# A two-layer trunk in one kernel: where residual tiles land, when prepared weight parts are made, and when attention's value products run

## The chip, the cores and the metric

The kernel is one program on one core of a Trainium2 chip. The time is the device time of one execution in microseconds (us). Before the change it is 2508.14 us, the median of three runs (2506.28 to 2510.22). In this document TensorE is the engine of the matrix products (PE in the profile), VectorE is DVE, ScalarE is ACT, GpSimd is POOL, and SyncE is SP, which here only issues transfers. PSUM is the memory that TensorE writes, SBUF the one from which all engines read.

## The reference

1024 tokens of width 1024 pass two layers. Each layer is a mixer, a multilayer perceptron (MLP) and a gated embedding (ple), each with a root-mean-square norm ahead of it and the residual added behind it. Layer 0's mixer is a gated spatial unit beside a gated delta rule; the change does not touch it. Layer 1's is differential attention with 8 heads, two sub-heads of 64 dimensions each, and values of 128. Cut to what matters:

```python
for layer in range(2):
    hn = rms_norm(h, ln_mix[layer])
    if layer == 0:
        h = h + concatenate([gmlp(hn), gated_delta(hn)]) @ w_out_e
    else:
        q, k, v = split(hn @ w_qkv_o)            # 8 heads; q, k normed per sub-head
        logits = q_r @ k_r.T - slope * dist      # r = 0, 1; causal
        attn = softmax(logits_0) - lam * softmax(logits_1)
        h = h + rms_norm(attn @ v) @ w_out_o
    hn = rms_norm(h, ln_mlp[layer])
    h = h + square(relu(hn @ w_mlp1[layer])) @ w_mlp2[layer]    # 1024 -> 4096 -> 1024
    gate = sigmoid(rms_norm(h, ln_ple[layer]) @ w_ple_gate[layer])
    h = h + (p[layer] @ w_ple_proj[layer]) * gate
```

All of it is in 32-bit floats.

## The kernel before

**Products.** Activations lie with the feature on the partitions, in tiles of 128 x 512: 8 tiles of features (m, or k where they are summed over), 2 halves of 512 tokens. Each operand x is split into two shorter numbers, hi = cast(x) on ACT and lo = x - hi on DVE (`split`, L265 and L269), and one product is three matmuls, hi·hi, hi·lo and lo·hi (`mm3`, which issues at L81; transposes are L84). A weight is loaded by SP into a `raw` buffer (8 of them, used in turn), its two parts go to `w` buffers (12, in turn). A buffer taken again waits for whoever still reads its old content.

**MLP.** Each of its two matrices is a 2 x 2 block product done with seven block products instead of eight. The first matrix runs in 8 chunks of columns: `front(0..4)` makes two products of chunks 0 to 4, `rest(0..4)` the other five of each of them, `chained(5..7)` all seven of the last three, with sums on DVE, relu and square on ACT. The hidden activations go to DRAM (`gd`). The second matrix is seven calls of `product2`, n = 1, 5, 6, 3, 7, 4, 2, each with 16 steps; a step loads 256 KB of weights (`raw` or `keep`) and 256 KB of `gd` (`graw`), splits both, and issues 12 matmuls of 128 x 512.

**Prepared parts.** Beside the first layer's MLP runs a generator, `prepare` (`side` in the code). One `next` of it is a step; there are 32, 8 heads by 4 pieces of the query and key weights. A step has POOL load a `raw` buffer (2 transfers of 128 KB, L243), ACT and DVE split it, and POOL store the two parts in DRAM (`qk_dram`, 256 KB each). Attention loads them from there. Eight steps run behind chunks 5 to 7 (3, 3 and 2), and 24 in the odd steps of the products n = 1, 4 and 2.

**Regions.** Large tiles have fixed places in SBUF, and one place serves many stages. A0 holds the values of two heads during attention; A2 and A3 the keys, of even and odd heads; A4, A5 and A1 the logits, in turn; c0 to c13 are 128 x 512 places, of which c8 to c10 hold `aT`, transposed probabilities. Afterwards A0 to A3 take the residual tiles `acc` of layer 1: 8 tiles of features for each half, four to a region.

**Attention.** The 64 blocks are 8 heads by 8 blocks of 128 queries. Step g of the loop issues, in this order: the logits of sub-head 0 of block g; the combination of the two probabilities of block g-1; transposes of the next queries (`put_q`); the transposes of block g-2 (`tr`, then a copy to `aT` on ACT); the logits of sub-head 1 of block g; the value products of block g-2 (`po`). Between these are four calls of `pump`, which put in other matmuls: projections of later heads' queries and keys (112 units), and from call 210 on the output matrix's sums over the first heads (`tails`, `mix_part`). KA = (5,5) says that the first five heads are summed there for each half of the tokens, in tiles `res` that are then written back to the residual in DRAM, `h_dram`. Behind the loop `mix_out` sums the other three heads: for each tile SP loads `acc` from `h_dram`, TensorE makes the sum, DVE adds it (L1496) and ACT squares it for the next norm.

**What sets the order.** The program's order is only the start: the tiling framework schedules the instructions with a simulation of its own and fixes each engine's order from that. SP and POOL take their transfers strictly in that order, so a transfer that waits for a buffer holds up all that stand behind it on the same engine.

Of the kernel before, what the change touches and what calls it, by code (L numbers as in the profile page):

```python
# [11 lines left out]
F32 = mybir.dt.float32  # L12
F32R = mybir.dt.float32r
AF = mybir.ActivationFunctionType
# [4 lines left out]
P = 128  # L19
# [4 lines left out]
HT = 512  # L24
# [4 lines left out]
WB = 12  # L29
EARLY = 3000  # L30
LAG = 3
KA = (5,5)
NQK = 112
MARKS = ((224, NQK),)
TAIL = 210
# [9 lines left out]
def f32(ap):  # L45
    return ap.bitcast(F32)
# [92 lines left out]
class Trunk:  # L139
# [192 lines left out]
    def mlp(self, x, x_tags, gain, w1, w2, gain_next, h_dram, p, last, side=iter(())):  # L332
        nc = self.nc
# [213 lines left out]
        t3, t2, make_t4, make_t1 = operands()  # L547
        for c in range(NCH):
            (rest if c < 5 else chained)(c)
            if c > 4:  # L550
                for _ in itertools.islice(side, 3 - (c == 7)):
                    pass
            if c + 2 in away:
                for i, t in enumerate(itertools.chain(*places(c + 2))):
                    nc.sync.dma_start(t, away[c + 2][i])
            elif c == 3:
                open1(5)
                open2(5)


        pT = self.split_p(p)
# [43 lines left out]
        def product2(n, ps, new=False, beside={}):  # L605

            for kt in range(NK):
                if kt in beside:
                    beside[kt]()
                if n in (1, 2, 4) and kt % 2:  # L610
                    next(side, None)
                a = self.parts(left(n, kt), nc.vector)
                raw = self.slot(f"c{next(raws)}", [P, HT], F32, "graw")
                load(raw, gd[n - 1][kt // 2][kt % 2])
                if n == 1 and kt < 4:
                    b = self.hs_parts(0, 4 + kt)
# [527 lines left out]
    def attention(self, w_qkv, v_dram, w_out, gain_next, h_dram):  # L1144

        nc = self.nc
        NB = NT
# [63 lines left out]
        lgs = [self.slot(t, [P, 2, S], F32, "lg") for t in ("A4", "A5", "A1")]  # L1211
        lg0, lg1 = ([x[:, r] for x in lgs] for r in range(2))
        qk_tag = itertools.cycle(("aux", "sc", "aux"))
        aT_tag = itertools.cycle(("c8", "c9", "c10"))
        heads = {}

        def begin(hd):

            qk = qks[hd]

            ks = self.slot(f"A{2 + hd % 2}", [P, 2, S], F32R, "ks")

            def put_k(hf):
                pt = self.aux([P, HT], "tr", "tr")
                for t in range(4):
                    self.pe.transpose(pt[:, t * P : (t + 1) * P], qk[1][hf][:, t, :], self.ident)
                for r in range(2):
                    own, other = half[r], half[1 - r]
                    dst = ks[:, r, hf * HT : (hf + 1) * HT]
                    nc.scalar.activation(dst[own], pt[own], AF.Copy, scale=self.kg[own])  # L1230
                    nc.vector.scalar_tensor_tensor(dst[other], pt[own], self.kg[own], f32(dst[own]), ALU.mult, ALU.subtract)

            def put_q(b2):
                pt = self.aux([P, HT], "tr", "tr")
                for i in range(2):
                    self.pe.transpose(pt[:, i * P : (i + 1) * P], qk[0][b2 // 2][:, 2 * (b2 % 2) + i, :], self.ident)
                qh = self.slot(f"c{11 + b2 % 2}", [P, 2, 2 * P], F32R, "qh")
                ql = qlow[b2 % 2]
                for r in range(2):
                    own, other = half[r], half[1 - r]  # L1240
                    g = self.qg[own, hd : hd + 1]
                    nc.scalar.activation(qh[own, r], pt[own, 0 : 2 * P], AF.Copy, scale=g)
                    nc.scalar.activation(qh[other, r], pt[own, 0 : 2 * P], AF.Copy, scale=g)
                    nc.vector.scalar_tensor_tensor(ql[own, r], pt[own, 0 : 2 * P], g, f32(qh[own, r]), ALU.mult, ALU.subtract)
                return qh, ql

            put_k(0)
            heads[hd] = [ks, put_k, put_q, put_q(0)]

        class Block:  # L1250
# [38 lines left out]
            def transpose(me):  # L1289
                me.aT = []  # L1290
                for c in range((me.n + HT - 1) // HT):
                    k0, k1 = 4 * c, min(me.b + 1, 4 * c + 4)
                    pt = self.aux([P, HT], "tr", "tr")
                    for k in range(k0, k1):
                        self.pe.transpose(pt[:, (k - k0) * P : (k - k0 + 1) * P], me.lg[0][:, k * P : (k + 1) * P], self.ident)
                    me.aT.append(self.slot(next(aT_tag), [P, HT], F32, "aT"))
                    nc.scalar.copy(me.aT[c][:, : (k1 - k0) * P], pt[:, : (k1 - k0) * P])  # L1297

            def value(me):
# [100 lines left out]

        tail = tails()
        blocks = []
        for g in range(8 * NB + 2):
            if g % NB == 2 and 0 < g // NB < 7:
                values(g // NB + 1)
            if g < 8 * NB:
                hd, b = divmod(g, NB)
                blocks.append(Block(hd, b))
                blocks[g].logits(0)
            if 0 < g <= 8 * NB:  # L1410
                blocks[g - 1].combine()
            pump()
            if g < 8 * NB and b % 2 and b < NB - 1:
                q = heads[hd][2]((b + 1) // 2)
            if g > 1:
                blocks[g - 2].transpose()
            pump()
            if g < 8 * NB:
                if b == 3 - (hd < 7):
                    heads[hd][1](1)  # L1420
                blocks[g].logits(1)
            pump()
            if g > 1:
# [832 lines left out]
def trunk(tc, x, p, ln_mix_e, w_in_e, gmlp_v_gain, gmlp_ws, gmlp_bs, gdn_conv, gdn_a_log, gdn_dt_bias, gdn_out_gain,  # L2256
          w_out_e, ln_mix_o, w_qkv_o, attn_q_gain, attn_k_gain, diff_lambda, attn_sub_gain, w_out_o, ln_mlp, w_mlp1,
          w_mlp2, ln_ple, w_ple_gate, w_ple_proj, masks, out):
    with ExitStack() as ctx:
# [60 lines left out]
        for layer in range(2):  # L2320
# [18 lines left out]
            acc, pT = T.mlp(x, (("A0", "A1") if layer else ("A1", "A0"), ("A2", "A3")), gain[3 * layer + 1], w_mlp1[layer], w_mlp2[layer], gain[3 * layer + 2], h_dram, p[layer, 0], layer == 1, T.prepare(w_qkv_o[0]) if layer == 0 else iter(()))  # L2339
# [50 lines left out]
```

## Time and profile before

| | us |
|---|---|
| median of three runs | 2508.14 (2506.28 to 2510.22) |
| the profiled execution | 2509.59 |
| its span, from the first to the last instruction | 2507.9 |
| TensorE busy in it | 2486.3 |
| DVE, ACT, POOL busy in it | 1828.3, 1347.9, 283.3 |

The mean TensorE clock granted in it is 0.998 of full speed. In the span, layer 0's mixer takes up to about 478 us, the first MLP's first matrix up to 790, its second up to 1101, the gated embedding and the values up to 1290, attention up to 1728, the rest of its output matrix up to 1768, the second MLP up to 2388, the last gated embedding up to 2508.

In rows of waits, `PE mm L81 <- DVE acc L1496: 4.7, 1, 4.7` would read: TensorE's matmuls into tiles `mm` waited 4.7 us in all, once, at most 4.7, and DVE's instruction at L1496 that writes `acc` ended that wait. In rows of windows the stretch comes first, then its length and the busy time (and count) of TensorE's matmuls, TensorE's weight loads, DVE, ACT and POOL, then the granted clock, the busy share of the 16 DMA engines and what they moved in GB/s. Rows of the chain give a start, a length, and the work in it. Rows of groups give the busy time, the mean length of one in ns, and the idle time ahead of them with who ended it. Ends of matmuls are modelled, so two in a row overlap in the rows.

### The profile page before, as it was taken

To read this page: it belongs to the slowest core of one execution; us is meant where nothing else is said; L and a number is where in the kernel's file an instruction comes from. 1 tells how busy PE (TensorE), PEld (TensorE's weight loads), DVE (VectorE), ACT (ScalarE), POOL (GpSimd) and SP (SyncE) were. 2 spreads that over 40 slices of the span, in tenths; PEclk is the share of its full clock that TensorE was granted. 3 is DMA by queue.
4 is the path that set the end of the run, shared out by engine and by line. 5 is a ranking of instruction groups with operands and counts; after the bars stand their busy time and mean duration, and the time that the engine had idled before them with its cause. 6 is when DMAs were issued, how large, how long until landed. Compare 5 with 4: busy or idle time off the path is not lost. (4 is left out here: it accounts for less than half of the span.)

```text
span 2507.9 us, 39353 instructions
## 1 busy us (share of the span) xinstructions
PE 2486.3 (99%) x13465; PEld 2112.4 (84%) x13465; DVE 1828.3 (73%) x3548; ACT 1347.9 (54%) x2734; POOL 283.3 (11%) x331
## 2 busy tenths in 40 slices
PE   9999999999999999999999999999999999999999
PEld 7898998888887888888889999987888888888887
DVE  7867665787666877766847787776887656788576
ACT  6635473655555444644527777764654555445452
POOL 0211220000023001410012333310000000000000
PEclk9999999999999999999999999999999999999999
DMA  8464445467569757964451221376467548656651
GB/s 237 129 183 106 151 124 168 158 215 242 182 232 354 268 165 231 314 187 147 149 182 54 89 73 60 132 238 195 154 219 227 189 163 294 202 186 205 198 175 64
DMA packets 326386, 454.05 MB, mean 181 GB/s; under 512 B 48836, under 2 KB 168104, under 8 KB 326184
## 3 DMA queue, kind: packets, MB, share of 16 engines
q1 hardware_dynamic: 317432, 425.82, 52.8%
q0 software_dynamic: 8192, 25.17, 3.0%
q8 instruction: 106, 1.74, 0.3%
q14 instruction: 96, 0.79, 0.1%
q10 hardware_dynamic: 560, 0.53, 0.1%
HBM read 318.23 MB, written 133.18 MB: 180 GB/s over the span
## 5 line engine op out<-in xcount | busy, mean ns | idle before, releaser
L81 PE MATMUL mm<-g,w 128*128 128x512 f32 x2592 | 603.2, 394 | 4.4 <-DVE g L269 4.4
L265 ACT CAST w<-raw 128x512 fp32r<-128x512 f32 (+1 forms) x588 | 359.8, 617 | 453.1 <-PE mm L81 381.7
L81 PEld LDWEIGHTS mm<-g,w 128*128 128x128 f32 x2592 | 487.6, 188 | 118.9 <-DVE g L269 5.2
L81 PE MATMUL mm<-hi,w 128*128 128x512 f32 x1728 | 554.5, 396 | 1.0 <-DVE g L339 0.7
L269 DVE TENSOR_TENSOR w<-raw,w 128x512 fp32r<-128x512 f32 (+1 forms) x588 | 399.2, 687 | 190.9 <-ACT w L265 168.1
L81 PE MATMUL mm<-w,hi 128*128 128x256 f32 (+2 forms) x2112 | 440.9, 302 | 1.4 <-DVE k L1195 0.9
L81 PEld LDWEIGHTS mm<-hi,w 128*128 128x128 f32 x1728 | 324.2, 188 | 76.0 <-ACT w L265 1.3
L81 PEld LDWEIGHTS mm<-w,hi 128*128 128x128 f32 x2112 | 339.2, 188 | 19.1 <-DVE k L1195 2.0
L81 PE MATMUL mm<-lo,w 128*128 128x512 f32 x864 | 340.3, 394 | 0.0
L81 PE MATMUL mm<-w,lo 128*128 128x256 f32 (+2 forms) x1056 | 316.2, 300 | 0.0
L81 PE MATMUL mm<-t,w 128*128 128x512 f32 x1152 | 271.3, 394 | 0.0
L81 PEld LDWEIGHTS mm<-t,w 128*128 128x128 f32 x1152 | 216.5, 188 | 50.5
L81 PEld LDWEIGHTS mm<-w,lo 128*128 128x128 f32 x1056 | 198.9, 188 | 7.9
L81 PEld LDWEIGHTS mm<-lo,w 128*128 128x128 f32 x864 | 162.5, 188 | 36.2
L269 DVE TENSOR_TENSOR g<-graw,g 128x512 fp32r<-128x512 f32 x216 | 148.1, 687 | 11.8 <-ACT g L265 6.1
L265 ACT CAST g<-graw 128x512 fp32r<-128x512 f32 x216 | 132.8, 618 | 37.6 <-PE mm L81 16.0
L310 POOL TENSOR_TENSOR r<-ms,mhalf 128x4 f32<-128x4 f32 x12 | 14.2, 1186 | 968.0 <-DVE ms L308 935.0
L1279 ACT ACTIVATE lg<-lg,nm 128x128 f32<-128x128 f32 (+7 forms) x128 | 99.4, 778 | 39.0 <-DVE nm L1276 37.9
L405 ACT ACTIVATE g<-g 128x512 f32<-128x512 f32 x100 | 63.1, 632 | 68.3 <-DVE g L339 68.0
L243 POOL DMA_DIRECT2D raw<-in_w_qkv_o_dram x64 | 46.4, 727 | 412.0 <-DMA gd<-v 207.5
L81 PE MATMUL mm<-ohi,w 128*128 128x512 f32 x256 | 86.6, 407 | 4.7 <-DVE acc L1496 4.7
L1276 DVE CUSTOM_DVE_ANT_0 lg<-qk,al 128x512 f32<-128x512 f32 (+3 forms) x128 | 74.4, 586 | 20.4 <-PE qk L81 18.3
(382 smaller groups left out, 3744.5 us busy)
## 6 DMA issues: line engine op xcount, KB each, us to landing
raw<-in_w_mlp_dram SPq DMA_DIRECT2D x352, 256.0 KB, 3.6
graw<-gd SPq DMA_DIRECT2D x224, 256.0 KB, 3.0
gd<-g SPq DMA_DIRECT2D x192, 256.0 KB, 3.6
raw<-in_w_ple_gate_dram SPq DMA_DIRECT2D x76, 256.0 KB, 3.6
acc<-h_dram SPq DMA_DIRECT2D x64, 256.0 KB, 5.0
qk_dram<-w POOLq DMA_DIRECT2D x64, 256.0 KB, 5.5
keep<-in_w_mlp_dram SPq DMA_DIRECT2D x64, 256.0 KB, 5.5
w<-qk_dram SPq DMA_DIRECT2D x64, 256.0 KB, 3.9
```

What stands on the lines that cost most here:

```text
L81: self._next(self.engine.matmul(*a, **k))
L243: self.nc.gpsimd.dma_start(raw[:, :, j * P : (j + 1) * P], w_qkv[2 * i * P : 2 * (i + 1) * P, c : c + P].rearrange("(k p) m -> p k m", p=P))
L265: inst = self.nc.scalar.copy(hi, src)
L269: inst = (lo_engine or self.nc.vector).tensor_tensor(lo, src, f32(hi), ALU.subtract)
L310: nc.gpsimd.tensor_tensor(r, ms, self.mhalf[:, 0:4], ALU.pow)
L405: nc.scalar.activation(g, src, AF.Relu)
L1276: nc.vector.tensor_tensor_reduce(out=lg[:, k0:k1], in0=ps[:, : k1 - k0], in1=al[:, u0 + k0 : u0 + k1], scale=-0.5 ** (hd + 1), scalar=3.0e ...
L1279: nc.scalar.activation(lg[:, :n], lg[:, :n], AF.Exp, bias=nm[:, r, nch - 1 : nch], scale=-1.0, accum_out=me.sums[:, b, r : r + 1])
```

## The change

It has four parts. Residual tiles: attention's output sums take the first six heads instead of five for half 0, and layer 1's residual tiles go to the regions A2, A0, A1, A3 in this order instead of A0, A1, A2, A3; the second MLP names the regions accordingly. Prepared parts: four steps behind each of chunks 1 to 4 of the first matrix (16), and 16 in the odd steps of the products n = 4 and 2; none behind chunks 5 to 7 and none in n = 1. Value products: those of block g-3 instead of g-2, issued ahead of the transposes of the next queries, with one more step of the loop, the load of the next head's values one step later, and five places instead of three for `aT` (two small places, rb0 and rb1, are added). Queries: in `put_q` the copies to the other half of the partitions come behind both first copies and their subtractions.

```diff
-KA = (5,5)
+KA = (6,5)
+ACC = "A2", "A0", "A1", "A3"
...
             (rest if c < 5 else chained)(c)
-            if c > 4:
-                for _ in itertools.islice(side, 3 - (c == 7)):
+            if 0 < c < 5:
+                for _ in itertools.islice(side, 4):
                     pass
...
-                if n in (1, 2, 4) and kt % 2:
+                if n in (2, 4) and kt % 2:
                     next(side, None)
...
-        aT_tag = itertools.cycle(("c8", "c9", "c10"))
+        aT_tag = itertools.cycle(("c8", "c9", "c10", "rb0", "rb1"))
...
                 for r in range(2):
-                    own, other = half[r], half[1 - r]
+                    own = half[r]
                     g = self.qg[own, hd : hd + 1]
                     nc.scalar.activation(qh[own, r], pt[own, 0 : 2 * P], AF.Copy, scale=g)
-                    nc.scalar.activation(qh[other, r], pt[own, 0 : 2 * P], AF.Copy, scale=g)
                     nc.vector.scalar_tensor_tensor(ql[own, r], pt[own, 0 : 2 * P], g, f32(qh[own, r]), ALU.mult, ALU.subtract)
+                for r in range(2):
+                    own = half[r]
+                    nc.scalar.activation(qh[half[1 - r], r], pt[own, 0 : 2 * P], AF.Copy, scale=self.qg[own, hd : hd + 1])
...
-        for g in range(8 * NB + 2):
-            if g % NB == 2 and 0 < g // NB < 7:
+        for g in range(8 * NB + 3):
+            if g % NB == 3 and 0 < g // NB < 7:
                 values(g // NB + 1)
...
             pump()
+            if g > 2:
+                blocks[g - 3].value()
             if g < 8 * NB and b % 2 and b < NB - 1:
                 q = heads[hd][2]((b + 1) // 2)
-            if g > 1:
+            if 1 < g < 8 * NB + 2:
                 blocks[g - 2].transpose()
...
-            if g > 1:
-                blocks[g - 2].value()
...
-                    accs[i] = T.slot(f"A{i}", [P, 4, HT], F32, "acc")
+                    accs[i] = T.slot((ACC[i] if layer else f"A{i}"), [P, 4, HT], F32, "acc")
...
-            acc, pT = T.mlp(x, (("A0", "A1") if layer else ("A1", "A0"), ("A2", "A3")), ...
+            acc, pT = T.mlp(x, ((ACC[0:2], ACC[2:4]) if layer else (("A1", "A0"), ("A2", "A3"))), ...
```

Three places show how the engines' orders move. The first is DVE at the prepared parts (buffers `w` and `raw`; a row's first name is the output). Before, at the passage from the first matrix to the second, w_8405 is such a part, between the weights of the product n = 1 (`keep`), its activations (`graw`) and the last sums of chunk 7 (L339):

```order
L269 TENSOR_TENSOR lo_8476<-graw_8473,hi_8475 128x512
L269 TENSOR_TENSOR w_8380<-keep_8377,w_8379 128x512
L339 TENSOR_TENSOR g_8069<-v_8073,mm_8214 128x512
L339 TENSOR_TENSOR g_7853<-g_8068,g_7853 128x512
L269 TENSOR_TENSOR w_8405<-raw_8401,w_8404 128x512
L269 TENSOR_TENSOR w_8413<-keep_8410,w_8412 128x512
L339 TENSOR_TENSOR g_8066<-u_7851,mm_8137 128x512
```

Now such parts (w_6517, w_6526, w_6535, w_6544) stand among the sums of the first matrix's chunks:

```order
L270 TENSOR_TENSOR w_6517<-raw_6513,w_6516 128x512
L340 TENSOR_TENSOR g_5567<-g_6260,g_5567 128x512
L340 TENSOR_TENSOR g_6261<-u_5566,mm_6296 128x512
L270 TENSOR_TENSOR w_6526<-raw_6522,w_6525 128x512
L340 TENSOR_TENSOR g_6262<-v_6264,mm_6413 128x512
L340 TENSOR_TENSOR g_5568<-g_6261,g_5568 128x512
L340 TENSOR_TENSOR raw_6568<-raw_6576,raw_6568 128x512
L270 TENSOR_TENSOR w_6535<-raw_6531,w_6534 128x512
L340 TENSOR_TENSOR raw_6576<-s_1187_6567,raw_6576 128x512
L270 TENSOR_TENSOR w_6544<-raw_6540,w_6543 128x512
```

The parts have left the row of loads and sums that the product n = 1 takes, and stand between sums that come in groups of a chunk.

The second is SP behind attention. Before, the tiles of A0 (acc_18989, the first four of half 0) stand last of the residual loads, behind those of A1 (acc_19071) and of half 1 (acc_19292), and behind the write of the last `res`:

```order
L1484 DMA acc_19292<-h_dram 128x512 x3
L387 DMA raw_19420<-in_w_mlp_dram 128x2x256
L1484 DMA acc_19071<-h_dram 128x512 x3
L1464 DMA h_dram<-res_18864 128x512
L1484 DMA acc_19071<-h_dram 128x512
L387 DMA raw_19422<-in_w_mlp_dram 128x2x256
L1484 DMA acc_19292<-h_dram 128x512
L1484 DMA acc_18989<-h_dram 128x512 x4
```

Now the first four of half 0 are acc_19007, in A2, issued some fifty rows earlier between the writes of half 0's sums; these are two of them:

```order
L1494 DMA acc_19007<-h_dram 128x512
L1474 DMA h_dram<-res_18200 128x512
L107 DMA raw_18857<-in_w_out_o_dram 128x2x256
L1461 DMA res_18727<-h_dram 128x512
L1461 DMA res_18353<-h_dram 128x512
L1494 DMA acc_19007<-h_dram 128x512
L1474 DMA h_dram<-res_18267 128x512
```

And the tiles of A0, now tiles 4 to 7 of half 0 (acc_19071), again stand behind the last `res`, with a tile of half 1 (acc_19280) behind them:

```order
L1494 DMA acc_19280<-h_dram 128x512
L388 DMA raw_19448<-in_w_mlp_dram 128x2x256
L1474 DMA h_dram<-res_18927 128x512
L1494 DMA acc_19071<-h_dram 128x512 x4
L1494 DMA acc_19280<-h_dram 128x512
L388 DMA raw_19450<-in_w_mlp_dram 128x2x256
```

So A0's loads keep their place on SP, but other tiles of the sum are in them.

The third is TensorE in attention, at a block of head 2: tr_14702 are transposes of probabilities, aT_14700 their first copy, po its value products, qk logits, mm a projection. Before:

```order
L84 MATMUL tr_14695<-ident,lg_13240 128x128 x4
L81 MATMUL qk_14711<-ks_13997,qh_14515 128x512
L81 MATMUL qk_14711<-ks_13997,ql_13236 128x512
L81 MATMUL mm_14770<-w_14604,hi_12040 128x256
L81 MATMUL mm_14770<-w_14603,lo_12041 128x256
L81 MATMUL mm_14770<-w_14603,hi_12044 128x256
L81 MATMUL mm_14770<-w_14604,hi_12044 128x256
L81 MATMUL mm_14770<-w_14603,lo_12045 128x256
L84 MATMUL tr_14702<-ident,lg_13240 128x128 x2
L81 MATMUL qk_14761<-ks_14649,qh_14662 128x128
L81 MATMUL qk_14761<-ks_14649,ql_13235 128x128
L81 MATMUL po_14735<-v_13242,aT_14700 128x128 x4
```

And now:

```order
L85 MATMUL tr_14695<-ident,lg_13240 128x128 x4
L82 MATMUL mm_14760<-w_14587,hi_12040 128x256
L82 MATMUL mm_14760<-w_14586,lo_12041 128x256
L82 MATMUL mm_14760<-w_14586,hi_12044 128x256
L82 MATMUL mm_14760<-w_14587,hi_12044 128x256
L82 MATMUL mm_14760<-w_14586,lo_12045 128x256
L82 MATMUL qk_14751<-ks_14639,qh_14652 128x128
L82 MATMUL qk_14751<-ks_14639,ql_13235 128x128
L85 MATMUL tr_14702<-ident,lg_13240 128x128 x2
L85 MATMUL tr_14735<-ident,o_14355 128x128 x4
L82 MATMUL po_14779<-v_13242,aT_14700 128x128 x4
```

Between the first transposes and the value products there are nine matmuls and two transposes before, seven matmuls and six transposes now: at this place the scheduler has left them about as close as they were.

More of the change, by code (lines that the diff above doesn't have):

```diff
@@ L1213, in attention, with aT_slot @@
         qk_tag = itertools.cycle(("aux", "sc", "aux"))
-        aT_tag = itertools.cycle(("c8", "c9", "c10"))
+        aT_tag = itertools.cycle(("c8", "c9", "c10", "rb0", "rb1"))
+        def aT_slot():
+            tag = next(aT_tag)
+            if tag[0] == "r":
+                return self.sp.tile([P, HT], F32, tag=tag, name=self.nm("aT"), bufs=1)
+            return self.slot(tag, [P, HT], F32, "aT")
         heads = {}
@@ L1295, in transpose @@
                         self.pe.transpose(pt[:, (k - k0) * P : (k - k0 + 1) * P], me.lg[0][:, k * P : (k + 1) * P], self.ident)
-                    me.aT.append(self.slot(next(aT_tag), [P, HT], F32, "aT"))
+                    me.aT.append(aT_slot())
                     nc.scalar.copy(me.aT[c][:, : (k1 - k0) * P], pt[:, : (k1 - k0) * P])
@@ L2338, in trunk @@
             T.wide = ("mm", "tr", "aux", "sc")
-            acc, pT = T.mlp(x, (("A0", "A1") if layer else ("A1", "A0"), ("A2", "A3")), gain[3 * layer + 1], w_mlp1[layer], w_mlp2[layer], gain[3 * layer + 2], h_dram, p[layer, 0], layer == 1, T.prepare(w_qkv_o[0]) if layer == 0 else iter(()))
+            acc, pT = T.mlp(x, ((ACC[0:2], ACC[2:4]) if layer else (("A1", "A0"), ("A2", "A3"))), gain[3 * layer + 1], w_mlp1[layer], w_mlp2[layer], gain[3 * layer + 2], h_dram, p[layer, 0], layer == 1, T.prepare(w_qkv_o[0]) if layer == 0 else iter(()))
             T.wide = ("mm", "sc" if layer else "tr")
```

## The prediction

> **What bounds the kernel now.** I read the page's first part, then what TensorE waited for over the whole run, then the windows around each wait, and last the chain of waits.
>
> ```profile
> span 2507.9 us, 39353 instructions
> PE 2486.3 (99%) x13465; PEld 2112.4 (84%) x13465; DVE 1828.3 (73%) x3548; ACT 1347.9 (54%) x2734; POOL 283.3 (11%) x331
> PE mm L81 <- DVE acc L1496: 4.7, 1, 4.7
> PE mm L81 <- DVE g L269: 4.4, 2, 3.7
> PE po L81 <- ACT aT L1297: 1.8, 6, 0.4
> PE tr L84 <- ACT aT L1297: 1.2, 2, 0.7
> PE mm L81 <- DVE k L1195: 0.9, 1, 0.9
> PE mm L81 <- DVE g L339: 0.7, 1, 0.7
> ```
>
> TensorE is busy 2486.3 of 2507.9 us: 21.6 us stand idle in the whole program, and the change neither adds nor removes a matmul. So it can only win waits back. Two waits stand out (4.7 and 4.4 us), the others are small and mostly in attention. But a wait costs more than its idle time, which the next rows show. They are 38 us windows, with TensorE's busy time and its count of matmuls first, and the granted clock, DMA share and GB/s last.
>
> ```profile
> 779.00:817.00 38.00, 33.64 (x138) 26.64 (x138) 25.99 (x43) 20.45 (x38) 6.93 (x13) 0.96 1.02 380
> 817.00:855.00 38.00, 38.00 (x166) 30.74 (x165) 31.33 (x52) 16.98 (x30) 0.67 (x2) 1.00 0.96 346
> 2042.00:2080.00 38.00, 38.00 (x166) 30.73 (x165) 23.54 (x38) 21.73 (x39) 0.00 (x0) 1.00 0.58 203
> 1789.26 292.29 PE mm L81 x1260
> L81 PE MATMUL mm<-g,w 128*128 128x512 f32 x2592 | 603.2, 394 | 4.4 <-DVE g L269 4.4
> 1526.70 0.77 PE tr L84 x7
> ```
>
> 779 to 817 is where the first MLP passes from its first matrix to its second. It holds 138 matmuls, a full window 166: 28 are missing. A row of the chain prices one: 292.29 / 1260 = 0.232 us (and a transpose 0.77 / 7 = 0.11). So 28 x 0.232 = 6.5 us are lost there, though only 4.4 show as idle: a matmul's modelled length is 0.394 us, so its end lies 0.16 us behind the next one's start, and the clock falls after the wait.
>
> ```profile
> 800.00:805.00 5.00, 1.29 (x4) 0.83 (x3) 4.01 (x7) 2.93 (x6) 1.09 (x2) 0.86 1.06 405
> 805.00:810.00 5.00, 5.00 (x19) 4.01 (x18) 2.83 (x5) 1.80 (x4) 1.08 (x2) 0.80 0.96 331
> DVE g L269 <- DMA gd<-g: 3.6, 1, 3.6
> ACT w L265 <- DMA keep<-in_w_mlp_dram: 3.7, 1, 3.7
> qk_dram<-w POOLq DMA_DIRECT2D x15, 256.0 KB, 6.0
> ```
>
> DVE and ACT were late there because transfers were: the DMA engines are full (share 1.06, 405 GB/s), and 15 of the transfers issued from 770 to 810 store prepared parts. The second MLP runs the same code with no prepared parts; its passage (2042 to 2080) loses nothing and moves 203 GB/s. The other large wait is behind attention. From the chain and two windows:
>
> ```profile
> 1728.02 4.15 DMA acc<-h_dram
> 1732.26 0.70 DVE acc L1496
> 1733.00 4.21 PE mm L81 x9
> 1737.21 0.85 PE tr L84 x4
> 1738.06 14.28 PE mm L81 x60
> 1728.00:1733.00 5.00, 0.31 (x2) 0.00 (x0) 0.92 (x3) 0.02 (x1) 2.25 (x3) 0.90 0.87 261
> 1733.00:1740.00 7.00, 7.00 (x21) 5.60 (x22) 2.12 (x3) 1.30 (x2) 0.00 (x0) 0.58 0.30 113
> ```
>
> After the last value product the residual tiles are loaded into A0, which held the heads' values until then; the first addition waits for that load, and TensorE for the addition, which frees its PSUM tile. Nine matmuls then take 4.21 us instead of 9 x 0.232 = 2.09: the granted clock is 0.58.
>
> **The change, part by part.** Sums are made against the profiled execution (2509.59 us, its span 2507.9). It lies 1.45 us above the median of the three runs, 2508.14.
>
> *Prepared parts taken out of the passage.* Eight of 32 steps leave the first product of the second matrix and eight the chunks ahead of it. What stays there is what the second MLP does without loss: -6.5 us. The least is 0, if the stage's own loads were the cause; the most is 6.5 plus the wait of 0.7 and its hidden 0.16, so -7.4. I take -6.5, since the identical code loses nothing.
>
> *Prepared parts put into chunks 1 to 4 of the first matrix.* A step is two loads of 128 KB and two stores of 256 KB on POOL's queue, a cast on ACT and a subtraction on DVE.
>
> ```profile
> 562.00:590.00 28.00, 28.00 (x123) 22.67 (x122) 21.17 (x36) 14.07 (x24) 0.00 (x0) 1.00 0.72 235
> 1793.00:1821.00 28.00, 28.00 (x122) 22.56 (x122) 28.00 (x47) 20.97 (x40) 0.00 (x0) 1.00 0.48 158
> L265 ACT CAST w<-raw 128x512 fp32r<-128x512 f32 (+1 forms) x588 | 359.8, 617 | 453.1 <-PE mm L81 381.7
> L269 DVE TENSOR_TENSOR w<-raw,w 128x512 fp32r<-128x512 f32 (+1 forms) x588 | 399.2, 687 | 190.9 <-ACT w L265 168.1
> q0 software_dynamic: 8192, 25.17, 3.0%
> DMA to landing us min/median/max: 2.3/5.5/7.8
> ```
>
> A chunk is five products of 24 matmuls: 120 x 0.232 = 27.8 us. Four steps add 4 x 0.687 = 2.7 us to DVE's 21.2 of 28, and 4 x 0.617 = 2.5 to ACT's 14.1. The second MLP has a window with DVE busy 28.00 of 28.00 and TensorE full, so both are covered. Transfers: POOL's queue moves 25.17 MB for 32 steps, 0.79 MB each; four in 27.8 us are 113 GB/s on top of 235, so 348. The window from 817 moved 346 with TensorE full, so I expect this to be hidden too, barely. A prepared buffer comes free only when its store has landed (5.5 us, at most 7.8); in the new order the next user on the same engine stands 10 to 17 instructions later, in the old one often 8. By 0.617 to 0.687 us each, that is 6 us or more, and 5 for the old. I take +0.5; the bounds are 0 and, for one disturbed chunk, the 6.5 that the passage lost. If the cover is gone, casts are late and TensorE's weights after them.
>
> The Trainium skill, "DMA: Bandwidth & Descriptors", section "Where 436 GB/s comes from", puts the HBM side at about 358 GB/s for a core, which would leave 348 almost no room. This trace differs (380 over 38 us, 405 over 5), and the measurement decides; by that rule all four chunks would stall, the first rival below.
>
> *Residual tiles into A2 first.* A2 holds the keys of head 6, done a head earlier, so SP can issue these four loads long before the end; A0's four loads stay behind the last value product, but are now needed only by output tiles 4 to 7. Lost now: 4.7 + 0.16 of wait, 4.21 - 2.09 = 2.12 in nine slow matmuls, 0.85 - 0.44 in transposes, 14.28 - 60 x 0.232 = 0.36: 7.75 us. What remains is the hand-over of a PSUM tile (an addition of 0.70 us behind two covering matmuls of 0.46, and the modelled end): about 0.5. And what is late next is head 7 itself:
>
> ```profile
> 1725.39 1.06 PE L81 MATMUL po<-v,aT 128*128 128x128 f32 x8
> 1729.77 1.04 POOL L1323 TENSOR_TENSOR o<-o,of 128x512 f32<-128x512 f32 x1
> ```
>
> From the last value product (1726.45) to POOL's scaling of its outputs (1730.81) it is 4.4 us, which the old wait hid; the new order has 18 matmuls, 4.2 us, ahead of their transposes. With half 0 at only 6 matmuls a tile (1.39 us) for DVE's addition and square sum, I leave another 0.5 for this. So -6.75; bounds 0 and -7.75.
>
> On the clock, the Trainium skill, "TensorE: Matmul & The Clock Gate", section "What's actually happening", has half rate end after about 3.4 us of sustained work. That would make the slow tail at most 1.7 us against 2.9 from the rows, and the forecast 1.2 us later; the granted 0.58 over 7 us speaks for the rows.
>
> *Six heads summed inside attention.* 24 matmuls (5.6 us) of half 0 move from behind attention into it: no change in TensorE's sum. Two loads, two casts and two subtractions go, beside TensorE: 0. They give the last blocks something to run between a transpose and its value product.
>
> *Value products a block step later, five transposed buffers, copies of q reordered.* Six value products waited for ACT's copy: 1.8 + 6 x 0.16 = 2.8 us, and transposes and a query, 1.2 + 0.4, for buffers or copies. The step alone doesn't fix the distance: the emitted order still brings some value products up to their transposes. With the matmul times above, pairs closer than 0.8 us fall from 8 of 96 to 3. I take half of 2.8, -1.5. Bounds: -6 (all of attention's waits, 4.3 shown in ten places with 0.16 each) and +6 (as many new ones, since DVE and ACT are reordered too and DVE is about 78% busy there).
>
> ```profile
> 1420.00:1520.00 100.00, 99.24 (x794) 95.64 (x793) 78.83 (x243) 76.07 (x194) 30.55 (x35) 1.00 0.25 80
> PE qk L81 <- ACT qh L1243: 0.4, 1, 0.4
> ```
>
> *Sum.* -6.5 + 0.5 - 6.75 - 1.5 = -14.25: 2509.59 - 14.25 = 2495.3 for a run like the profiled one, 2493.9 at the median. I forecast **2494 us**.
>
> **Rivals.**
> *The chunks stall (ends slower).* 348 GB/s is a mean, and bursts of loads and saves reach the 405 at which the passage stalled. If each of the four chunks loses what the passage lost, 4 x 6.5 = 26 replace the 0.5: 2519 us. From three chunks on the gain is gone (2513). For it: share 0.72 with 235 GB/s scales to 1.06 at 348. Against: 0.96 and 346 without loss, and weights of the chunks are loaded far ahead. Chance 0.05.
> *The passage stalls anyway*, from its own saves, loads and residual tiles (ACT and DVE waited for `gd` and `keep`, none of them prepared parts): 2494 + 6.5 = 2500.5. Against: the second MLP. Chance 0.08.
> *The wait behind attention only moves* to A0's tiles, or DVE becomes the bound there: two additions and squares per 1.39 us, and SP holds A0's loads behind a write of the last residual sums. Then most of 6.75 stays: 2500.5. Chance 0.10.
> *Attention gets new waits* of the size of its old ones instead of fewer: +6 + 1.5, 2501.5. Chance 0.07.
> *Attention loses nearly all its waits*: 2494 - 4.5 = 2489.5. Chance 0.12.
>
> **How the numbers follow.** The forecast, 2491 to 2498, has 0.58. The range is **2488 to 2502**: it takes in the three rivals around 2500 and the better attention, and leaves out the stalling chunks and pairs of rivals. A measurement of this kernel tells 0.2% from no change, 5 us: faster means under 2503.1. Forecast, the better attention and each single middle rival are faster, 0.95 together; two of those together (2507 and more) come to some 0.05, taken from them. Faster 0.90, same 0.05, slower 0.05.
>
> **What would show it.** Right: no wait of mm for g L269 near 800, and a 38 us window there with about 166 matmuls at clock 1.00; prepared parts' stores between 570 and 690 at 300 to 350 GB/s, TensorE full; no wait over 1 us for the residual additions, and no window under 0.9 clock behind attention; fewer waits of po for aT. Wrong: missing matmuls between 560 and 690 with casts waiting for loads or buffers; the second group of residual additions waiting for its load; waits of qk or tr in attention beyond 6 us in all.

## The result and the profile after

The changed kernel takes 2490.45 us (median of four runs, 2489.38 to 2491.46); the kernel before, run beside it, 2508.51. The ratio is 0.9928 with an interval of 0.9911 to 0.9946: 18 us faster. The forecast was 2494 us, with a range of 2488 to 2502. A second set on another chip (`f_after` below) gave 2490.80 and 0.9922, 0.9908 to 0.9936.

The first part of the page, and waits of TensorE on which the argument rests, in the changed kernel:

```profile
span 2487.3 us, 39296 instructions
PE 2476.5 (100%) x13465; PEld 2109.8 (85%) x13465; DVE 1828.6 (74%) x3546; ACT 1341.6 (54%) x2732; POOL 284.2 (11%) x331
PE qk L82 <- ACT qh L1254: 1.3, 2, 1.1
PE aux L82 <- POOL r L311: 0.9, 1, 0.9
PE tr L85 <- POOL o L1333: 0.9, 1, 0.9
PE po L82 <- ACT t L1319: 0.8, 1, 0.8
PE mm L82 <- DVE acc L1506: 0.3, 1, 0.3
```

Both large waits (4.7 and 4.4 us) are gone, and so are the six of value products for `aT`. Two are new: queries wait for `qh`, the copies that were put last, and the norm behind attention for POOL. Idle time fell from 21.6 us to 10.8.

The windows of the prediction, in the changed kernel (TensorE's busy time and matmuls first; granted clock, DMA share and GB/s last):

```profile
562.00:590.00 28.00, 28.00 (x123) 22.74 (x122) 22.82 (x38) 15.75 (x28) 10.12 (x16) 1.00 0.95 332
590.00:618.00 28.00, 28.00 (x123) 22.77 (x122) 25.81 (x44) 15.67 (x28) 10.12 (x16) 1.00 0.99 354
779.00:817.00 38.00, 38.00 (x166) 30.82 (x165) 24.80 (x40) 17.44 (x31) 0.00 (x0) 1.00 0.89 305
1733.00:1740.00 7.00, 6.93 (x34) 5.40 (x33) 6.89 (x13) 5.02 (x10) 0.00 (x0) 1.00 0.79 264
```

The passage holds 166 matmuls instead of 138 and moves 305 GB/s instead of 380. The chunks carry the prepared parts at 332 and 354 GB/s and lose no matmul. Behind attention the clock is 1.00, where it was 0.58.

To compare kernels whose matmuls stand in another order I added up, in three stretches, how much later each matmul starts after the one before it than is usual for a pair of their sizes (usual: the first quartile over the traces of the kernel before, the changed one and `f_old_q`). A level of about 1 in the first stretch and 23 in the second is what remains when nothing large waits; only differences count. The last two columns are read directly: the start of the last matmul of the first MLP, and the time from there to the first one of the second MLP's second matrix. The 23.0 and 18.7 us in the expectation of e3_values took each trace's own median as usual, so their level is another one.

| trace | passage, from 740 | first query to last value product | 45 us behind it | end of first MLP | from there to the second MLP's second matrix |
|---|---|---|---|---|---|
| before | 8.3 | 29.2 | 9.4 | 1097.1 | 997.1 |
| changed | 1.1 | 23.2 | 3.0 | 1088.7 | 985.4 |
| e1_prepared | 1.1 | 29.2 | 7.3 | 1090.0 | 994.4 |
| e2_tiles | 8.6 | 28.1 | 12.3 | 1097.1 | 999.1 |
| e3_values | 11.7 | 24.2 | 8.1 | 1100.7 | 992.0 |
| e5_tiles_order | 9.3 | 28.7 | 7.6 | 1097.8 | 994.9 |
| e6_no_step | 1.1 | 30.9 | 12.4 | 1090.1 | 1004.0 |
| f_old_q | 1.1 | 22.7 | 1.2 | 1090.1 | 981.3 |

The kernel before, e2, e3 and e5 have the same order of instructions up to attention, so their four passages are four draws of one thing: 8.3, 8.6, 11.7 and 9.3.

### The profile page after: what moved, and what is told of

It reads as the page before. It is cut to its first block, busy times and chain, and to the rows that moved or that the text cites. A ratio compares the mean times of both kernels' runs of the same rounds, so it can differ in the third digit from the quotient of the medians.

```text
span 2487.3 us, 39296 instructions
## 1 busy us (share of the span) xinstructions
PE 2476.5 (100%) x13465; PEld 2109.8 (85%) x13465; DVE 1828.6 (74%) x3546; ACT 1341.6 (54%) x2732; POOL 284.2 (11%) x331
## 4 chain that ended last, share of the span: by engine, by line
PE 98%; DVE 1%; ACT 0%; issue 0%; DMA 0%; POOL 0%; ACTq 0%; DVEq 0%; POOLq 0%
PE mm L82 85%; PE po L82 3%; PE qk L82 3%; PE tr L85 2%; PE aux L82 2%; DVE lg L1286 0%; PE pks L82 0%; PE pkq L82 0%; PE pvn L82 0%; PE pkk L82 0%; PE pgm L82 0%; PE pab L85 0%; PE pst L82 0%; DMA x<-in_x_dram 0%; PE aux L85 0%
## 5 line engine op out<-in xcount | busy, mean ns | idle before, releaser
L266 ACT CAST w<-raw 128x512 fp32r<-128x512 f32 x586 | 357.7, 617 | 427.9 <-PE mm L82 371.5
L270 DVE TENSOR_TENSOR w<-raw,w 128x512 fp32r<-128x512 f32 x586 | 398.3, 687 | 181.8 <-ACT w L266 165.8
L1289 ACT ACTIVATE lg<-lg,nm 128x256 f32<-128x256 f32 (+7 forms) x128 | 99.3, 776 | 41.2 <-DVE nm L1286 40.3
```

The source lines that it names most:

```text
L266: inst = self.nc.scalar.copy(hi, src)
L270: inst = (lo_engine or self.nc.vector).tensor_tensor(lo, src, f32(hi), ALU.subtract)
L1289: nc.scalar.activation(lg[:, :n], lg[:, :n], AF.Exp, bias=nm[:, r, nch - 1 : nch], scale=-1.0, accum_out=me.sums[:, b, r : r + 1])
```

## The experiments

### The three parts alone

Each is the kernel before with one part of the diff.

> The kernel before with only the prepared parts moved (four steps behind chunks 1 to 4, none behind 5 to 7 and none in the product n = 1). By the prediction the window 779 to 817 us holds 166 matmuls instead of 138 and the wait of mm for g is gone: 6.5 to 7.4 us less, 2501 us. Rival one, the passage's own loads and saves were the cause: no gain, 2508. Rival two, the three parts of the change need each other (the gain of the whole comes only together): less than half of it here. The wait behind attention (4.7 us for L1506 or so) must stay.

```diff
-            if c > 4:
-                for _ in itertools.islice(side, 3 - (c == 7)):
+            if 0 < c < 5:
+                for _ in itertools.islice(side, 4):
...
-                if n in (1, 2, 4) and kt % 2:
+                if n in (2, 4) and kt % 2:
```

Measured: 2498.88 us against 2508.99, ratio 0.9962 (0.9949 to 0.9976): 10.1 us, the forecast gain and more. In its trace:

```profile
779.00:817.00 38.00, 38.00 (x165) 30.80 (x164) 25.59 (x41) 17.68 (x31) 0.00 (x0) 1.00 0.87 297
1725.00:1732.00 7.00, 7.00 (x27) 5.63 (x28) 2.81 (x4) 1.23 (x3) 0.00 (x0) 0.80 0.31 114
```

The part needs no other. Why 10 and not 6.5: the profile of before was the mildest draw of the passage (e3's, with the same order, lost 3.4 us more), and this trace also lost 2.1 us less behind attention. There its order is that of before, the wait is 3.7 instead of 4.7 us, and in the 7 us after it the clock was granted at 0.80 here (second row) and at 0.58 before. I take this second difference for chance and not for the part's doing; there is one trace of each kernel, so that is not shown.

> The kernel before with only the residual tiles changed: six heads summed for half 0 inside attention and the order A2, A0, A1, A3. By the prediction 6.75 us less, 2501.5 us, and no wait of mm for acc over 1 us, clock 1.00 in 1733 to 1740. Rival: the wait moves to the tiles of A0 or to head 7's last outputs, which POOL scales 4.4 us after the last value product: then 2 us or less is gained, 2506. The passage at 779 to 817 must still lose 6.5.

```diff
-KA = (5,5)
+KA = (6,5)
+ACC = "A2", "A0", "A1", "A3"
...
-                    accs[i] = T.slot(f"A{i}", [P, 4, HT], F32, "acc")
+                    accs[i] = T.slot((ACC[i] if layer else f"A{i}"), [P, 4, HT], F32, "acc")
...
```

The same edit names the regions accordingly where the second MLP is called.

Measured: 2513.62 us, ratio 1.0021 (1.0012 to 1.0030): slower. A part that was to win 6.75 us costs 4.6 when it comes alone. Two sets of rows say why. First, from the timeline and from SP's own waits in 1700 to 1760 us:

```profile
1728.52 1.06 PE L82 MATMUL po<-v,aT 128*128 128x128 f32 x8
1732.35 2.22 SPq L1485 DMA_DIRECT2D acc<-h_dram  x5
1737.80 0.69 DVE L1497 TENSOR_TENSOR acc<-acc,mm 128x512 f32<-128x512 f32 x1 [5.34 <-DMA acc<-h_dram]
SPq L1485 <- DMA h_dram<-res: 8.1, 3, 4.1
```

The last value product ends at 1729.6, but the five loads of the second row are issued from 1732.4 on. The first of them is a load of half 1 that reads a row of `h_dram` just written from `res`; such loads wait up to 4.1 us for a write to land (last row), and A0's four loads wait behind this one. And A0 is not needed late: the third addition in DVE's order is already one of its tiles. DVE waits 5.34 us. Second, what TensorE waits for behind that:

```profile
PE mm L82 <- DVE acc L1497: 4.1, 2, 3.7
PE aux L82 <- POOL r L311: 2.1, 1, 2.1
PE aux L82 <- DVE sqs L293: 1.2, 1, 1.2
```

`aux` is the norm of half 0: a matmul over the sums of squares (`sqs`), a power on POOL (`r`), a matmul that spreads it. In the kernel before and in the changed one the scheduler has put an output tile of 9 matmuls between the two; here it has put them side by side, so the way over DVE and POOL is open.

> The kernel of e2_tiles with one thing more: the four loads of half 1's last residual tiles (into A3) are ordered behind the four loads into A0. In e2_tiles one of them stood ahead of A0's on SP and waited 4.1 us for the write of the row that it reads. If that order is what kept the gain away, the loss from 1728 to 1768 us (11.9 there, 8.4 in the kernel before) falls to 3 or less and the time is 2500 to 2503 us. If the residual tiles can't win anything without the later value products (A0's tile is the third that is added in either case, and its load takes 5 us from the last value product), it stays at 2508 or more.

```diff
                 a = place[m] = acc(m)
-                nc.sync.dma_start(a, h_dram[m, :, cols])
+                load = nc.sync.dma_start(a, h_dram[m, :, cols])
+                if h == 0 and m == 7:
+                    self.last_a0 = load.ins.name
+                if h == 1 and k0 and m >= 4:
+                    self.pe.behind(load, self.last_a0)
```

Measured: 2508.04 us against 2509.54, ratio 0.9991 (0.9982 to 1.0000). The time falls on the second expectation (2508 or more), the loss behind attention, 7.6 us, on neither, and the rows separate two causes:

```profile
1729.88 1.06 PE L82 MATMUL po<-v,aT 128*128 128x128 f32 x8
1730.97 2.24 SPq L1485 DMA_DIRECT2D acc<-h_dram  x5
PE mm L82 <- DVE acc L1501: 0.3, 1, 0.3
PE aux L82 <- POOL r L311: 2.1, 1, 2.1
PE aux L82 <- DVE sqs L293: 1.2, 1, 1.2
1733.00:1740.00 7.00, 6.89 (x32) 5.58 (x33) 3.42 (x8) 1.32 (x2) 2.25 (x3) 1.00 0.92 296
1755.00:1768.00 13.00, 10.06 (x42) 8.59 (x43) 9.00 (x16) 5.52 (x11) 1.01 (x1) 0.74 0.25 84
```

With A0's loads ahead they are issued at once, the wait for `acc` falls from 4.1 to 0.3 us and the clock in 1733 to 1740 is 1.00. So the order on SP was one cause; loss behind attention falls from 12.3 to 7.6. Whether the tiles win anything over the kernel before without the later value products is not shown: 7.6 us stand against 9.4 there, but 7.3 in e1_prepared, whose order is that of before. The norm's waits stay, and the clock from 1755 to 1768 is 0.74; by these rows that is most of what is left. TensorE's order there in this kernel:

```
L82 MATMUL mm_19314<-ohi_18991,w_19277 128x512
L82 MATMUL aux_19124<-ones_87,sqs_19017 128x1
L82 MATMUL aux_19133<-ident_82,r_19131 128x128
L82 MATMUL mm_19298<-ohi_18969,w_19264 128x512
```

In the changed kernel the nine matmuls of mm_19314 stand between the two `aux`. That the neighbourhood of the two is the cause is read from these rows; it was not undone by itself.

> The kernel before with only the attention loop changed: value products a step later, five places for aT, copies of q reordered. By the prediction 1.5 us less inside attention, 2507 us. Rival, from the trace of the changed kernel (loss in attention 23.0 us before, 18.7 after, counted from the starts of its matmuls): 4 us less, 2504. Second rival: the six heads summed inside, not the loop, brought the 4.3, then 0 to 1 here.

The edit is the diff of the attention loop, of `aT_slot` and of `put_q`. Measured: 2505.24 us, ratio 0.9988 (0.9979 to 0.9997), 3.8 us. Its trace lost 5.0 us less between the first query and the last value product (24.2 against 29.2), and its passage was the worst of the four draws. The time alone, with some 0.8 to 5.3 us in its interval, leaves the forecast 1.5 open; the trace speaks for the first rival, and against the second, since five heads are summed here as before. The six waits for `aT` have shrunk to one of 0.3 us:

```profile
PE po L81 <- ACT aT L1306: 0.3, 1, 0.3
PE qk L81 <- ACT qh L1253: 1.3, 2, 1.1
PE po L81 <- ACT t L1318: 0.8, 1, 0.8
```

Alone the parts give -10.1, +4.6 and -3.8 us, in sum -9.3; together they give -18.1. By the table most of the difference lies behind attention: there the parts alone change the loss by -2.1, +2.9 and -1.3 us, together by -6.4. With the value products a step later, the scheduler happens to put A0's loads ahead of that load of half 1 and a tile between the two matmuls of the norm.

### The step, the copies and the places

> The changed kernel with the value products back at block g-2 (five aT places and the reordered copies of q stay). By the reading that the step itself took the waits of po for aT away, these are back: 2 to 4 us more inside attention. Moreover the scheduler has put a load of half 1 behind the last written row ahead of A0's loads on SP, as in e2_tiles: if that order costs what it seems to cost there, 4 to 6 us more behind attention, together 2497 to 2500 us. If only the number of aT places counts and the order on SP doesn't, it stays at 2490 to 2492.

The edit takes the loop's part of the diff back. Measured: 2510.78 us, ratio 1.0006 (0.9997 to 1.0015): 20 us above the changed kernel, two to three times what was expected; the whole gain is gone although the passage stays clean (166 matmuls).

```profile
PE mm L82 <- DVE acc L1506: 3.2, 2, 2.9
PE aux L82 <- POOL r L311: 2.1, 1, 2.1
PE po L82 <- ACT aT L1307: 2.1, 5, 1.0
PE aux L82 <- DVE sqs L293: 1.3, 1, 1.3
```

Three losses are back at once: the products wait for `aT` again (attention 30.9 against 23.2, more than was expected), A0's loads stand behind the load of half 1 again, and the norm's matmuls side by side (12.4 against 3.0). So the gain of the residual tiles hung on the step, by way of the scheduler's order.

The gain inside attention is the step's as well. Counted as in the table, but by the tile whose matmul starts late, 37 of the 576 matmuls of value products start more than 0.05 us late before, 5.8 us together; in the changed kernel it is 10 and 1.9 us, and here, with five places but without the step, 29 and 5.4 us.

> The changed kernel with the copies of q in their old order. In the changed kernel TensorE waits 1.3 us for qh, the second copies of L1254 which now come last; before it waited 0.4. If the reorder brought only these waits, they go and the time is 1 to 2 us less, 2488.5 to 2489.5. If it made transposes and subtractions of the next queries earlier and so carries part of the gain in attention, the time is 1 to 3 us more, 2491.5 to 2493.5.

The edit takes the change in `put_q` back. Measured: 2487.60 us (2486.41 to 2488.86), 2.9 us below the changed kernel's median from the earlier set; ratio to before 0.9912 (0.9898 to 0.9925). The reorder had cost time. The next two sets were made for this.

> The changed kernel again, beside the next two on one chip: 2489.4 to 2491.5 as before if the chip makes no difference.

Measured: 2490.80 us (2489.87 to 2491.34).

> The changed kernel with the copies of q in their old order (e7_old_q again), to compare with f_after on the same chip. If the 2.9 us between the medians of e7_old_q and the changed kernel are the waits for qh (1.3 us with their hidden parts) and the wait for the norm behind attention (1.0 us), it is 2 to 4 us below f_after. If they were a difference of chips, within 1 us of it.

Measured beside it: 2486.94 us (2485.97 to 2487.78), 3.9 us below, the ranges well apart; ratio to before 0.9907 (0.9893 to 0.9921). It is the best kernel of this study. From 1310 to 1712 us its TensorE waits, in all, for:

```profile
PE tr L85 <- POOL o L1331: 0.9, 1, 0.9
PE mm L82 <- DVE k L1196: 0.2, 1, 0.2
```

The waits for `qh` are gone; and the norm's wait behind attention (0.9 us on POOL's `r` in the changed kernel) is gone as well: 3.0 to 1.2 in the table. The first is the direct effect, the second again one of order. The table places 2.3 of the 4.1 us by which its last column falls (985.4 to 981.3); the rest lies in starts that it takes for usual.

> As f_old_q with three places for aT instead of five. Blocks 4 to 7 of a head need two places each, so with three the transposes of a block have to wait for the value products of the one before. If the places matter, TensorE's transposes wait for value products and ACT's copies come late: 3 us or more above f_old_q. If only the step matters, within 1 us of it.

Measured: 2489.14 us (2488.74 to 2491.34), 2.2 us above f_old_q: between the two expectations. Its ACT waits 2.4 us in one place for a value product to free an `aT` place:

```profile
ACT aT L1298 <- PE po L82: 2.4, 1, 2.4
```

In attention it lost only 0.8 us more than f_old_q (23.5 against 22.7), behind it 1.7 (2.9 against 1.2). So the places count a little, and the later step carries most of the gain.

### What makes the passage late

> The changed kernel with 16 stores of 256 KB more on POOL's queue beside the first eight steps of the product n = 1 of the first MLP, from the weights that this product has loaded; nothing reads what they write, and no engine computes more. If transfers alone make the passage late, matmuls are missing again from 779 to 817 (4 to 7 us lost, 138 to 150 of 166) with the DMA engines' share near 1. If it was the casts, the subtractions or the turn of the w buffers, nothing is lost (under 1 us).

```diff
                 a = self.parts(left(n, kt), nc.vector)
+                if n == 1 and kt < 8 and not last:
+                    for _ in range(2):
+                        junk = self.dp.tile([P, HT], F32, name=self.nm("junk"))
+                        nc.gpsimd.dma_start(junk, f32(keep[0, kt][:, 0]))
```

> The changed kernel with 16 pairs of a cast on ACT and a subtraction on DVE more, at the places where the kernel before makes prepared parts (3, 3 and 2 behind chunks 5 to 7, 8 in the odd steps of n = 1), from an operand that lies in SBUF, into w buffers that nothing reads; no transfers. If transfers alone made the passage late, as x_stores says (6.0 us lost there with stores alone), 740 to 817 us loses under 1 us. If the engines' work or the turn of the w buffers also does it, 2 us or more.

```diff
+        def extra():
+            self.parts(f32(t2[0][0]).rearrange("p (k m) -> p k m", m=256), nc.vector)
...
+            if c > 4 and not last:
+                for _ in range(3 - (c == 7)):
+                    extra()
...
+                if n == 1 and kt % 2 and not last:
+                    extra()
```

The window of the passage, of x_stores and then of x_casts, and x_stores' longest wait:

```profile
779.00:817.00 38.00, 33.88 (x140) 27.05 (x139) 22.08 (x35) 15.30 (x27) 2.15 (x4) 0.96 0.99 363
PE mm L82 <- DVE g L270: 4.1, 1, 4.1
```

```profile
779.00:817.00 38.00, 38.00 (x165) 30.77 (x164) 28.81 (x47) 20.64 (x38) 0.00 (x0) 1.00 0.91 308
```

Stores alone bring nearly the whole loss back: 140 matmuls, the wait of `mm` for `g` of 4.1 us (4.4 before), the clock at 0.96; the single time is 2495.93 us, 5.5 above the changed kernel. Casts and subtractions alone, with DVE busier than before (28.8 against 26.0 us), lose nothing there; the single time is 2492.06 us. So transfers alone are enough to make the passage late, and the engines' work alone does nothing. What neither run tries alone is a `w` buffer that stays taken until its store has landed. x_stores issues its stores on POOL, and the transfer that came late, a store of `g` to `gd` for which DVE waited 3.8 us, is SP's. The Trainium skill, "DMA: Bandwidth & Descriptors", section "Issuing engines are not separate DMA queues", says that transfers of all issuing engines share the same 16 DMA engines; this pair agrees.

### How much a chunk bears

> The changed kernel with eight prepared steps instead of four behind each of chunks 1 to 4, and none left for the products n = 4 and 2. Eight steps of 0.79 MB in 27.8 us are 226 GB/s on top of 235, together 461. If the transfers bound it at the 405 GB/s that the passage of the kernel before reached, a chunk of 12.8 MB takes 31.6 us instead of 27.8, some 15 us lost between 562 and 700. If steps spread into later chunks since POOL waits for the casts, less: 5 us. If a chunk bears it, under 1 us.

The edit is `islice(side, 8)` for `islice(side, 4)`. Measured once: 2543.66 us, 53 above the changed kernel, more than any of the expectations.

```profile
562.00:590.00 28.00, 17.70 (x69) 13.52 (x69) 19.15 (x31) 13.98 (x24) 10.65 (x20) 0.83 0.97 350
646.00:674.00 28.00, 22.83 (x87) 17.71 (x87) 16.98 (x27) 13.82 (x24) 9.41 (x18) 0.88 0.99 359
PE mm L82 <- ACT w L266: 37.0, 5, 10.9
raw<-in_w_mlp_dram SPq DMA_DIRECT2D x5, 256.0 KB, 9.1
SPq L411 <- ACT g L407: 59.5, 10, 22.7
```

The first rival is real at eight steps: TensorE waits for weights five times, up to 10.9 us, and of the 123 and 122 matmuls that the changed kernel has in the two windows 54 and 35 are missing. At four steps none was; where between the two the loss begins was not measured. The bytes do not explain the size, and my 15 us counted bytes only. Two other things stand in the trace. Loads of weights land late: after 9.1 us in the median of five issued from 572 to 587 (last row but one), where three in the changed kernel land after 6.9 in the same window and nothing is lost. And SP itself stands still: from 562 to 702 it waits 59.5 us, up to 22.7 at a time, to store activations that ACT has not made yet (last row; 15.8 us in the changed kernel), and loads of weights stand behind these stores. Which of the two makes the size, and which follows from the other, stays open.

## Why the prediction was right, and where it was off

**What bounds.** Right: TensorE's work did not change, and the gain is waits won back; its idle time fell by 10.8 us and the span by 20.6, so that a wait cost more than its idle time, as the prediction said, here about twice.

**Passage (-6.5).** Right in place and cause: x_stores and x_casts show that transfers are enough, and the bound of zero ("the stage's own loads were the cause") is excluded by e1. Mis-sized: the four draws lose 7.2, 7.5, 10.6 and 8.2 us above the changed kernel's level. I took the size from one trace, and it was the mildest.

**Chunks (+0.5).** It is nothing measurable: 123 matmuls per 28 us at 332 and 354 GB/s. The Trainium skill's figure of some 358 GB/s for the HBM side ("DMA: Bandwidth & Descriptors", section "Where 436 GB/s comes from"), which I had set beside 348, did not make the chunks stall, and 380 over 38 us in the passage of before lie above it; where it does stall (x_eight) 350 to 359 are moved over 28 us. The rival was rightly named and rightly thought unlikely at four steps; at eight it cost far more than bytes give.

**Residual tiles (-6.75).** The amount is about right (9.4 to 3.0, or 7.3 to 3.0 from e1's trace), the reasoning is not. The step that failed is "A0's four loads stay behind the last value product, but are now needed only by output tiles 4 to 7": the third addition is A0's, the tiles are worked on in another order than counted. What is won comes from A0's loads standing directly behind the last value product on SP. In the changed kernel:

```profile
1713.84 1.95 PE L82 MATMUL po<-v,aT 128*128 128x128 f32 x16
1715.82 3.37 SPq L1494 DMA_DIRECT2D acc<-h_dram  x5
1721.52 0.69 DVE L1506 TENSOR_TENSOR acc<-acc,mm 128x512 f32<-128x512 f32 x1 [1.54 <-DMA acc<-h_dram]
```

From the first of these issues to the addition it is still 5.7 us; two early tiles, 18 matmuls and free PSUM tiles cover it, and DVE waits 1.54 us, TensorE 0.3. The rival that I gave 0.10 (the wait only moves to A0's tiles, and SP holds A0's loads behind a write of the last residual sums) is what e2 does, and what the changed kernel escapes by the order of two rows. I did not derive that order, so that the term came out near its size is luck. And the norm, by the rows the most of what e5 loses more than the changed kernel (7.6 against 3.0 us), was in no rival.

**Six heads (0).** e2 lost 1.1 and e5 0.5 us less in attention (28.1 and 28.7 against 29.2): a small gain that I had left out.

**Value products (-1.5).** The clearest mis-sized term: attention lost 6.0 us less (29.2 to 23.2), at my bound of -6, and e3 by itself won 5.0. I added up the rows of waits and took half. But the rows of waits in attention hardly moved, 4.3 us in all before and 3.6 in the changed kernel (1.3, 0.9, 0.8 and, of `mm` for `k`, 0.6). What went are late starts too small for a row: 37 of value products, of which only six show as waits. In the same part the reordered copies of q cost 3.9 us, which I had not priced apart: they bring 1.3 us of waits for `qh` and, through the order, the norm's wait.

**Sum.** Corrected terms: -7.2 to -10.6 (passage), 0, -4.3 to -6.4 (tiles), -6.0 (attention), together -17.5 to -23.0; measured -18.1. The forecast came 3.5 us too high in time, mostly by the value products; the range held it in its lower part, between the forecast's own 2491 and the 2489.5 of the rival of the better attention.

## What to carry to other kernels

Where a scheduler sets the order, parts of a change don't add up: here +4.6, -3.8 and -10.1 gave -18.1, since one load that stood ahead of four others on SP was worth 4.7 us, and one tile between two matmuls of a norm, by the rows, most of 4.6. So read the emitted order at every hand-over behind the edit, above all which transfer that waits for a write stands ahead of a critical load. Size a wait from several traces if an unchanged stretch can give them, and do not price transfers beside critical loads by bytes alone: look also at when loads land and at how long the engine that issues them stands.

## What the runs showed of the hardware that I had not expected

- The same instructions in the same order lost between 7.2 and 10.6 us in the passage from trace to trace, with the DMA engines' share at 1.01 to 1.03 from 779 to 817. Elsewhere stretches repeat: the last column of the table is 985.4 in both traces of the changed kernel.
- After waits of 3.7 and 4.7 us in the same place the mean clock over 7 us was 0.80 in one trace (1725 to 1732 of e1_prepared) and 0.58 in the other (1733 to 1740 of before): the price of a wait is not a constant. Narrower windows show half clock in both, but for some 6.8 us in before (first two rows) and some 3.4 in e1_prepared:

```profile
1732.10:1738.80 6.70, 5.80 (x16) 4.63 (x17) 2.06 (x3) 1.32 (x2) 0.00 (x0) 0.50 0.31 118
1738.90:1745.00 6.10, 6.10 (x28) 4.97 (x27) 3.91 (x6) 2.35 (x4) 0.00 (x0) 1.00 0.34 125
1724.50:1727.80 3.30, 3.01 (x7) 2.46 (x8) 0.92 (x2) 0.63 (x1) 0.00 (x0) 0.50 0.43 163
1727.90:1732.00 4.10, 4.10 (x21) 3.34 (x20) 2.13 (x3) 0.83 (x2) 0.00 (x0) 1.00 0.19 67
```

  By these rows 3.4 us more at half clock cost about 1.7 us while TensorE has work (an estimate), most of the 2.1 us between the two traces. In the passage half clock lasts some 3.4 us in before (0.50 from 803.7 to 807.0) and some 6.8 in e3 (0.50 from 804.8 to 811.5), the worst of the four draws. The Trainium skill, "TensorE: Matmul & The Clock Gate", section "What's actually happening", has half rate end after at least one window of about 3.4 us of sustained work; the traces agree, with one such length and with two. The prediction's "at most 1.7 us" by that section counts one window; the slow tail here held two.
- Weights loaded from 572 to 587 land after 9.1 us in x_eight, after 6.9 in the changed kernel, with a share of 0.95 to 0.97 from 562 to 590 in both; TensorE lost 50 us in the one before the second matrix (its first matmul starts at 840.0, in f_after at 789.7) and none in the other. What x_eight moved there are 16 more steps of 0.79 MB, 12.6 MB.
